# First-stage shift and scale from one-column matmuls, and seven units in the first stage instead of three

## The chip, the core and the metric

The kernel runs on one core of one Trainium2 chip. The core has a matrix engine (TensorE, PE in the rows; PEld is its loading of weights), a vector engine (VectorE, DVE), a scalar engine (ScalarE, ACT), GpSimd (POOL) and a queue that issues transfers (SyncE, SP). Each has its own instruction queue and runs it in order. The metric is device time in microseconds, from launch to end.

## The reference, cut to what matters

A decoder block of 256 tokens and width 2048: an FFN, a token mixer and a second FFN, each fed by a normed input that a shift and a scale modulate. All nine modulation vectors are one vector-matrix product.

```python
c_act = jax.nn.silu(c)                       # c: (1, 2048)
mod = c_act @ w_ada[l] + b_ada[l]            # w_ada: (2048, 9 * 2048)
sh1, sc1, g1, sh2, sc2, g2, sh3, sc3, g3 = jnp.split(mod, N_MOD, axis=-1)

h = modulate(rmsnorm(x, norm1_w[l]), sh1, sc1)        # rmsnorm(x) * (1 + sc1) + sh1
x = x + 0.5 * g1[:, None, :] * swiglu(h, ffn1_gate[l], ffn1_up[l], ffn1_down[l])
...
```

## The kernel before, in words

Everything is float32. A matmul of activations with a weight is made exact enough by splitting both operands into two float32r parts (`hi`, `lo`) and adding three products (lines 239 to 241). Weights come as panels `w` of 128 partitions x 1024 columns (two blocks of 128 rows by 512 output columns, 512 KB). For each panel ACT writes the `hi` half (L214) and DVE the `lo` half (L215) of a tile `hl`. A **unit** is a pair of PSUM banks (two token tiles) for one chunk of 512 gate or up columns; a **step** of a unit is one panel: 12 matmuls of 512 columns.

The transposed, modulated input `h` is needed in blocks of 128 features, and its shift (`s_col`) and scale (`a_col`) depend on `w_ada`. So the first FFN starts in **stages** of feature blocks, `STAGES = ((0, 2), (2, 4), (4, 8), (8, 12), (12, 16))`: stage s first needs the shift and scale of its blocks, then works through its units on those blocks alone. Partial sums stay in PSUM (`carry`), or are copied out by ACT to `part` (L517) and added to by DVE later (L524).

Shift and scale of a block come from `dot_panel` (L98): a 512 KB panel `at` of transposed `w_ada` (features on partitions, half of the 2048 inputs along the row) is multiplied with the row `crow` = silu(c) on DVE and summed along the row (L101). Two vectors, two halves: four panels to a block, eight for a stage of two blocks. `col_fin` (L105) adds halves, bias and 1 (L110 to L113). `crow` itself is made by four matmuls that spread one row over 128 partitions (`cb`, L89) and a Silu on ACT (L90).

`h_pre` normalises and transposes (tiles `xn`, `hx`, L307 and L312), `h_post` applies scale and shift and splits (L324, L325 on ACT, L328 on DVE).

What sets the order: a `Feed` queue holds the dot panels of the next stage; `mm_unit` pops some behind each weight panel, by a rate, and `next_stage` drains it but for two, issues the first weight panel of the next stage, and flushes the last two. All raw panels (`w`, `at`) share one ring of 7 buffers, all issued by SP in program order: an issue waits until its buffer was read. Split tiles `hl` have 5 buffers.

Stage 0 works on three units (the first two of `pairs` in reverse, and `res`), which stay in PSUM; rate is 0 there, so all eight dot panels of stage 1 are popped by `next_stage`. Stage 1 takes these three one step further and then eight more units two steps each. In all 3 + 19 = 22 steps.

Of the kernel before, what the change touches and what calls it, by code (L numbers as in the profile page):

```python
# [7 lines left out]
F32 = mybir.dt.float32  # L8
# [18 lines left out]
BEHIND = (3, 8, 16)  # L27
CARRY = 2
DEFER, YDEFER = 2, 4
# [13 lines left out]
def decoder_block(  # L43
    ctx: ExitStack,
    tc: tile.TileContext,
    x_in, c_t, c_r, ada_t, ada_g, b_row, b_col, norm_c, gate1, up1, down1, w_in, pool_w, pool_c,
    lb_c, gnorm, w_out, gate2, up2, down2, fin_w, ident_c, lmask_c, pcnt_c, out,
# [14 lines left out]

# [1 line left out]
    ccol = const.tile([P, KB], F32, name="ccol")  # L64
# [6 lines left out]
    ident = const.tile([P, P], F32, name="ident")  # L71
    nc.sync.dma_start(out=ident, in_=ident_c)
    bcol = const.tile([P, 9 * KB], F32, name="bcol")
    nc.sync.dma_start(out=bcol, in_=b_col)
    ncol = const.tile([P, 3 * KB], F32, name="ncol")
    nc.sync.dma_start(out=ncol, in_=norm_c)
    ones = const.tile([P, P], F32, name="ones")
# [17 lines left out]

# [1 line left out]
    # shift and scale: output features on partitions, one dot product over c per partition  # L97
    def dot_panel(vec, blk, half):  # L98
        raw = wraw.tile([P, AW], F32, tag="raw", name=f"at{vec}_{blk}_{half}")
        nc.sync.dma_start(out=raw, in_=ada_t[COLS.index(vec), blk, half])  # L100
        nc.vector.scalar_tensor_tensor(  # L101
            raw, raw, 1.0, crow[:, half * AW:(half + 1) * AW], ALU.mult, ALU.mult,
            accum_out=dots[:, COLS.index(vec), blk, half:half + 1])

    def col_fin(vec, b0, b1):  # L105
# [8 lines left out]

    # gates: input features on partitions, partial products summed over partitions by PE into every row
    def row_step(vec, half, k, box):
# [23 lines left out]
    class Feed:  # L140
# [3 lines left out]
        def add_blocks(self, vecs, b0, b1):  # L144
# [4 lines left out]
            for vec in vecs:  # L149
                self.q.append((0, lambda v=vec: col_fin(v, b0, b1), vecs[-1]))  # L150

        def add_row(self, vec):
            def begin():
                self.g[vec] = state.tile([P, D], F32, tag="g", name=f"g{vec}")
            self.q.append((0, begin, vec))
            for h in range(2):
                box = {}
                for k in range(KB):
                    self.q.append((1, lambda h=h, k=k, box=box: row_step(vec, h, k, box), vec))
                self.q.append((0, lambda h=h, box=box: row_fin(vec, h, box, self.g[vec]), vec))  # L160
# [22 lines left out]

# [1 line left out]
    cnt = [0]  # L185
# [35 lines left out]
    def mm_unit(ps, steps, rate, lag=0, first=True, last=True):  # L221
        """ps[t] = sum over steps (lhs(t) parts, panel source); token tile 1 trails by lag steps of 2 K blocks"""
        n = len(steps)
        held = {}
        if ahead:
            held[0] = ahead.pop()
        for i in range(n + lag):
            for t in range(NT):
                j = i - lag * t
                if not 0 <= j < n:  # L230
                    continue
                if j not in held:
                    held[j] = panel(steps[j][1], rate, lag > 0 and j % 3 == 2)
                if len(steps[j]) > 2:
                    ensure(steps[j][2])
                for b, (wh, wl) in enumerate(held[j]):
                    xh, xl = steps[j][0](b, t)
                    st, sp = first and j == 0 and b == 0, last and j == n - 1 and b == 1
                    nc.tensor.matmul(ps[t], xh, wh, start=st, stop=False)  # L239
                    nc.tensor.matmul(ps[t], xh, wl, start=False, stop=False)  # L240
                    nc.tensor.matmul(ps[t], xl, wh, start=False, stop=sp)  # L241
# [13 lines left out]

# [1 line left out]
    def rsqrt(ssq, n, denom, bias, name):  # L257
        """-2 / sqrt(ssq / denom + bias), the square root of ACT refined by a Newton step"""
        r = small.tile([P, n], F32, tag="rr", name=f"rr_{name}")
        m = small.tile([P, n], F32, tag="rq", name=f"rq_{name}")  # L260
        u = small.tile([P, n], F32, tag="ru", name=f"ru_{name}")
        a = nc.scalar.activation(r, ssq, AF.Sqrt, bias=bias, scale=1.0 / denom)
        nc.vector.tensor_scalar(m, ssq, 1.0 / denom, bias, ALU.mult, ALU.add)
        nc.vector.reciprocal(r, r)
        if n > 1:
            nc.vector.tensor_tensor(u, r, r, ALU.mult)
            nc.vector.tensor_tensor(u, u, m, ALU.mult)
        else:
# [23 lines left out]

# [48 lines left out]

# [1 line left out]
    def split_slot(slot, b, ps):  # L343
# [3 lines left out]
    def project(w, srcs, g_t, rate, name, y=None, first=False, ssq=None, then=None, post=None, need=None):  # L347
        """g_t given: x += g * (y + srcs @ w), then(t); else y (+)= srcs @ w"""
        rs = {}
# [50 lines left out]

# [1 line left out]
    def hid_chunk(name, sl, up, defer):  # L402
        """sl[t] <- sl[t] * up[t], transposed and split into a slot"""
        slot = slots.tile([P, 2, 4, S], F32R, tag="sl", name=f"hid{name}")
# [42 lines left out]

# [1 line left out]
    ssq = new_ssq("0")  # L449
    rstd = {}  # L450
    for t in range(NT):
        for n in range(4):
            add_ssq(ssq, t, n, n * CW, CW)
        rstd[t] = row_rstd(ssq, t, row_bias(ssq, t, "0"), "0", 3)
        nc.vector.tensor_scalar(rstd[t], rstd[t], -0.5, None, ALU.mult)

    def stage_pre(st):
        k0, k1 = STAGES[st]
        return [([k, k + 1], h_pre(0, rstd, [k, k + 1], [0, 1], True)) for k in range(k0, k1, 2)]

    pre = stage_pre(0)
    feed.add_blocks((1, 0), *STAGES[0])

    def next_stage(c, i, k):
        """the rest of the modulation that the next stage needs, its first weight panel a little before the end"""
        feed.drain(AHEAD)
        ahead.append(panel((gate1, up1)[i][c, k // 2], 0))
        feed.flush()
# [4 lines left out]
    def order(s):  # L473
        fin = s == len(STAGES) - 1
        units = pairs[::-1] if (len(STAGES) - s) % 2 == 0 else list(pairs)
        if s == 0:
            units = units[::-1][:CARRY]
        keep = [] if fin else units if s == 0 else units[-CARRY:]
        return units + res if fin or s == 0 else units[:CARRY] + res + units[CARRY:], keep

# [3 lines left out]
    for s, (k0, k1) in enumerate(STAGES):  # L484
# [9 lines left out]
        else:  # L494
            feed.add_blocks((1, 0), *STAGES[s + 1])
            rate = 2 * sum(c for c, _, _ in feed.q) / sum(k1 - at.get(u, 0) for u in units) if s else 0
        for c, i in units:
# [45 lines left out]

# [1 line left out]
    feed.add_row(8)  # L545
# [33 lines left out]
    def to_feat(src, name):  # L579
        """two [tok, 512] tiles -> two PSUM banks [feat, 2 blocks, tok]"""  # L580
        res = []
# [16 lines left out]
    def hgrn(g):  # L598
# [23 lines left out]
        def col_sums(ps, k_ap, q_ap, name, i):  # L622
            """every row of ps = sums over the partitions of k * q"""
            pr = tmp.tile([P, CW], F32, tag="ev", name=f"pr{g}_{name}")
# [134 lines left out]

# [1 line left out]
    ssq = new_ssq("3")  # L761
# [4 lines left out]
    def finish(t, rs):  # L766
        for n in (1, 0, 2, 3):
# [13 lines left out]

_NAMES = ["x", "c_t", "c_r", "ada_t", "ada_g", "b_row", "b_col", "norm_c", "gate1", "up1", "down1", "w_in", "pool_w", "pool_c",
          "lb_c", "gnorm", "w_out", "gate2", "up2", "down2", "fin_w", "ident", "lmask", "pcnt"]
# [59 lines left out]
```

## Time and profile before

| | |
|---|---|
| median of 3 runs | 1874.09 us (1873.69 to 1875.05) |
| the profiled execution: span | 1872.2 us |
| median less span (launch, end) | 1.9 us |
| PE busy | 1838.7 us (98% of the span) |
| DVE busy, ACT busy | 1368.6 us, 866.1 us |
| read from memory | 491.28 MB |
| first matmul of stage 0, of stage 1, of stage 2 | 26.33, 41.50, 97.35 us |

The span runs from the first to the last instruction of the one profiled execution; the times of runs lie about 1.9 us above it. PE's share is high because a matmul is counted from its start to the end of its pipeline, and the next starts before that end.

### The profile page before, as it was taken

To read this page: it belongs to the slowest core of one execution; us is meant where nothing else is said; L and a number is where in the kernel's file an instruction comes from. 1 tells how busy PE (TensorE), PEld (TensorE's weight loads), DVE (VectorE), ACT (ScalarE), POOL (GpSimd) and SP (SyncE) were. 2 spreads that over 40 slices of the span, in tenths; PEclk is the share of its full clock that TensorE was granted. 3 is DMA by queue.
4 is the path that set the end of the run, shared out by engine and by line. 5 is a ranking of instruction groups with operands and counts; after the bars stand their busy time and mean duration, and the time that the engine had idled before them with its cause. 6 is when DMAs were issued, how large, how long until landed. Compare 5 with 4: busy or idle time off the path is not lost.

```text
span 1872.2 us, 22892 instructions
## 1 busy us (share of the span) xinstructions
PE 1838.7 (98%) x8348; PEld 1516.6 (81%) x8348; DVE 1368.6 (73%) x1721; ACT 866.1 (46%) x1085; POOL 6.5 (0%) x12
## 2 busy tenths in 40 slices
PE   5999999999999999999999999999999999999997
PEld 3878888888888888788888887888888888888886
DVE  6789898778888778898898859875444444454466
ACT  5554555444434444644535446444444444334443
POOL 0000000000000000000000000000000000000000
PEclk9999999999999999999999999999999999999999
DMA  9999988999999998477868857996555555555552
GB/s 365 328 332 333 307 265 316 341 341 331 329 335 340 337 333 292 156 268 268 317 251 316 274 205 250 323 330 204 189 192 198 190 183 189 193 196 189 187 192 90
DMA packets 137678, 494.89 MB, mean 264 GB/s; under 512 B 15831, under 2 KB 17367, under 8 KB 137181
## 3 DMA queue, kind: packets, MB, share of 16 engines
q1 hardware_dynamic: 137566, 493.44, 75.2%
q8 instruction: 65, 1.06, 0.2%
q14 instruction: 47, 0.39, 0.1%
HBM read 491.28 MB, written 2.10 MB: 264 GB/s over the span
## 4 chain that ended last, share of the span: by engine, by line
PE 97%; DVE 2%; ACT 0%; issue 0%; DMA 0%; SPq 0%; DVEq 0%; ACTq 0%
PE d L241 8%; PE d L240 8%; PE d L239 8%; PE u L241 7%; PE u L239 7%; PE u L240 7%; PE g L240 6%; PE g L239 6%; PE g L241 6%; PE s L241 4%; PE s L239 4%; PE s L240 4%; PE wo L240 2%; PE wo L239 2%; PE wo L241 2%; PE ht L413 1%
## 5 line engine op out<-in xcount | busy, mean ns | idle before, releaser
L215 DVE TENSOR_TENSOR hl<-w,hl 128x1024 fp32r<-128x1024 f32 x640 | 779.4, 1222 | 416.0 <-ACT hl L214 414.4
L214 ACT CAST hl<-w 128x1024 fp32r<-128x1024 f32 x640 | 672.5, 1055 | 828.6 <-PE d L241 219.6
L239 PE MATMUL d<-hl,hid 128*128 128x512 f32 x704 | 274.5, 390 | 0.0
L240 PE MATMUL d<-hl,hid 128*128 128x512 f32 x704 | 274.0, 389 | 0.0
L241 PE MATMUL d<-hl,hid 128*128 128x512 f32 x704 | 274.0, 389 | 0.0
L101 DVE SCALAR_TENSOR_TENSOR at<-at,crow 128x1024 f32<-128x1024 f32 x192 | 233.1, 1217 | 1.5 <-DMA at<-in_ada_t 1.5
L239 PE MATMUL u<-hl,h 128*128 128x512 f32 x544 | 211.6, 389 | 0.0
L240 PE MATMUL u<-hl,h 128*128 128x512 f32 x544 | 211.6, 389 | 0.0
L241 PE MATMUL u<-hl,h 128*128 128x512 f32 x544 | 211.6, 389 | 0.0
L239 PE MATMUL g<-hl,h 128*128 128x512 f32 x512 | 200.6, 392 | 0.0
L240 PE MATMUL g<-hl,h 128*128 128x512 f32 x512 | 199.6, 390 | 0.0
L241 PE MATMUL g<-hl,h 128*128 128x512 f32 x512 | 199.3, 390 | 0.0
L241 PEld LDWEIGHTS d<-hl,hid 128*128 128x128 f32 x704 | 132.1, 188 | 27.6
L240 PEld LDWEIGHTS d<-hl,hid 128*128 128x128 f32 x704 | 132.2, 188 | 27.2
L239 PEld LDWEIGHTS d<-hl,hid 128*128 128x128 f32 x704 | 132.1, 188 | 27.1
L239 PE MATMUL s<-hl,h 128*128 128x512 f32 x320 | 127.3, 398 | 12.3 <-ACT h L324 12.3
L240 PE MATMUL s<-hl,h 128*128 128x512 f32 x320 | 126.2, 394 | 0.0
L125 DVE SCALAR_TENSOR_TENSOR acc<-ag,ccol,acc 128x1024 f32<-128x1024 f32 x96 | 122.7, 1278 | 4.1 <-DMA ag<-in_ada_g 3.6
L241 PE MATMUL s<-hl,h 128*128 128x512 f32 x320 | 124.7, 395 | 0.9 <-DVE h L328 0.9
L240 PEld LDWEIGHTS u<-hl,h 128*128 128x128 f32 x544 | 102.1, 188 | 21.2
L241 PEld LDWEIGHTS u<-hl,h 128*128 128x128 f32 x544 | 102.1, 188 | 21.2
L239 PEld LDWEIGHTS u<-hl,h 128*128 128x128 f32 x544 | 102.1, 188 | 21.2
(247 smaller groups left out, 2035.6 us busy)
## 6 DMA issues: line engine op xcount, KB each, us to landing
at<-in_ada_t SPq DMA_DIRECT2D x192, 512.0 KB, 5.3
w<-in_up SPq DMA_DIRECT2D x176, 512.0 KB, 4.5
w<-in_gate SPq DMA_DIRECT2D x176, 512.0 KB, 4.7
w<-in_down SPq DMA_DIRECT2D x176, 512.0 KB, 3.8
ag<-in_ada_g SPq DMA_DIRECT2D x96, 512.0 KB, 5.1
w<-in_w_in SPq DMA_DIRECT2D x80, 512.0 KB, 4.7
w<-in_w_out SPq DMA_DIRECT2D x32, 512.0 KB, 4.5
x_sb<-in_x SPq DMA_DIRECT2D x2, 1024.0 KB, 7.0
```

Source lines behind the costliest of these rows:

```text
L101: nc.vector.scalar_tensor_tensor(raw, raw, 1.0, crow[:, half * AW:(half + 1) * AW], ALU.mult, ALU.mult, accum_out=dots[:, COLS.index(vec), ...
L125: nc.vector.scalar_tensor_tensor(acc, raw, ccol[:, k:k + 1], acc, ALU.mult, ALU.add)
L214: nc.scalar.copy(hl[:, 0], raw)
L215: nc.vector.tensor_tensor(hl[:, 1], raw, hl[:, 0].bitcast(F32), ALU.subtract)
L239: nc.tensor.matmul(ps[t], xh, wh, start=st, stop=False)
L240: nc.tensor.matmul(ps[t], xh, wl, start=False, stop=False)
L241: nc.tensor.matmul(ps[t], xl, wh, start=False, stop=sp)
L413: nc.tensor.transpose(ps[:, i, t * P:(t + 1) * P], sl[t][:, (b + i) * P:(b + i + 1) * P], ident)
```

## The change

Shift and scale of the first stage's two blocks are computed on TensorE: panels `as` (plain `w_ada` blocks, eight of 512 KB like before) serve as weights for one-column matmuls with a column of `ccol` = silu(c), 8 to a panel and 16 accumulated for each of four columns (2 vectors x 2 blocks) of one PSUM tile `a0`. `crow` is still made, for the later stages. Stage 0 takes seven units: four that are copied out to `part` afterwards (`SPILL`), then `res`, then the two that stay in PSUM. Stage 1 then has 15 steps instead of 19 (7 + 15 = 22), and its feed rate applies in stage 0 as well. Beside that, three small transfers are issued by ACT instead of SP, the second token tile's squares are summed by DVE in two instructions of 1024 instead of four on ACT, and one square root serves both tiles.

```diff
-CARRY = 2
+CARRY, SPILL = 2, 4
...
-    nc.sync.dma_start(out=ident, in_=ident_c)
+    nc.scalar.dma_start(out=ident, in_=ident_c)
...
+    first_ps = ps_ms.tile([P, 2, STAGES[0][1]], F32, tag="ms", name="a0")
+
+    def dot_pe(vi, blk, half):
+        raw = wraw.tile([P, KB // 2, P], F32, tag="raw", name=f"as{vi}_{blk}_{half}")
+        nc.sync.dma_start(out=raw, in_=ada_s[vi, blk, half])
+        for i in range(KB // 2):
+            k = half * (KB // 2) + i
+            nc.tensor.matmul(first_ps[:, vi, blk:blk + 1], raw[:, i, :], ccol[:, k:k + 1],
+                             start=k == 0, stop=k == KB - 1)
+
+    def col_fin_pe(vi, vec):
+        n = STAGES[0][1]
+        res = (s_col if vec == 0 else a_col)[:, 0, 0:n]
+        nc.vector.tensor_tensor(res, first_ps[:, vi, :], bcol[:, vec * KB:vec * KB + n], ALU.add)
+        if vec == 1:
+            nc.vector.scalar_tensor_tensor(res, res, 1.0, ncol[:, 0:n], ALU.add, ALU.mult)
...
-    rstd = {}
-    for t in range(NT):
-        for n in range(4):
-            add_ssq(ssq, t, n, n * CW, CW)
-        rstd[t] = row_rstd(ssq, t, row_bias(ssq, t, "0"), "0", 3)
-        nc.vector.tensor_scalar(rstd[t], rstd[t], -0.5, None, ALU.mult)
+    for n in range(4):
+        add_ssq(ssq, 0, n, n * CW, CW)
+    for n in range(2):
+        junk = slots.tile([P, 2, AW], F32, tag="sl", name=f"sq{n}")
+        xs = x_sb[:, 1, n * AW:(n + 1) * AW]
+        nc.vector.scalar_tensor_tensor(junk[:, 0], xs, 1.0, xs, ALU.mult, ALU.mult, accum_out=ssq[:, 1, n:n + 1])
...
+    feed.add_first()
+    feed.drain(4)
     pre = stage_pre(0)
-    feed.add_blocks((1, 0), *STAGES[0])
...
         if s == 0:
-            units = units[::-1][:CARRY]
-        keep = [] if fin else units if s == 0 else units[-CARRY:]
-        return units + res if fin or s == 0 else units[:CARRY] + res + units[CARRY:], keep
+            units = units[::-1]
+            return units[CARRY:CARRY + SPILL] + res + units[:CARRY], units[:CARRY]
+        keep = [] if fin else units[-CARRY:]
+        return units + res if fin else units[:CARRY] + res + units[CARRY:], keep
...
-            rate = 2 * sum(c for c, _, _ in feed.q) / sum(k1 - at.get(u, 0) for u in units) if s else 0
+            rate = 2 * sum(c for c, _, _ in feed.q) / sum(k1 - at.get(u, 0) for u in units)
```

The order of TensorE's queue at the start of the program, before (`cb` are the matmuls that spread c, `hx` the transposes, `s` the units; a row's x4 or x8 counts equal instructions in sequence):

```order
L89 MATMUL cb_117<-c_87,ones 128x512
L312 MATMUL hx_0_0_166<-ident,xn_0_0_165 128x128 x4
L239 MATMUL s_4_1_0_213<-hl_193,h_0_164 128x512
L240 MATMUL s_4_1_0_213<-hl_193,h_0_164 128x512
L239 MATMUL s_4_1_1_214<-hl_193,h_0_164 128x512
```

And after the change (`a` is the PSUM tile of the shifts and scales, `as` its panels of `w_ada`):

```order
L89 MATMUL cb_117<-c_87,ones 128x512
L113 MATMUL a_123<-ccol,as_0_0_150 128x1 x8
L113 MATMUL a_123<-ccol,as_0_1_160 128x1 x8
L113 MATMUL a_123<-ccol,as_1_0_170 128x1 x8
L337 MATMUL hx_0_0_192<-ident,xn_0_0_191 128x128 x4
L113 MATMUL a_123<-ccol,as_1_1_180 128x1 x8
L113 MATMUL a_123<-ccol,as_0_0_201 128x1 x8
L113 MATMUL a_123<-ccol,as_0_1_211 128x1 x8
L113 MATMUL a_123<-ccol,as_1_0_226 128x1 x8
L113 MATMUL a_123<-ccol,as_1_1_236 128x1 x8
L264 MATMUL s_3_1_0_253<-hl_223,h_0_190 128x512
```

64 one-column matmuls stand between the last `cb` and the first matmul of a unit, in the place of nothing but the transposes.

The order of VectorE's queue where stage 0 ends, before (from the split of the third unit's panel to the split of `h` for stage 1):

```order
L215 TENSOR_TENSOR hl_250<-w_248,hl_250 128x1024
L101 SCALAR_TENSOR_TENSOR at_2_1_277,dots<-at_2_1_277,crow 128x1024
L101 SCALAR_TENSOR_TENSOR at_2_0_280,dots<-at_2_0_280,crow 128x1024
L101 SCALAR_TENSOR_TENSOR at_2_1_283,dots<-at_2_1_283,crow 128x1024
L101 SCALAR_TENSOR_TENSOR at_3_0_286,dots<-at_3_0_286,crow 128x1024
L101 SCALAR_TENSOR_TENSOR at_3_1_289,dots<-at_3_1_289,crow 128x1024
L110 TENSOR_TENSOR a_col<-dots 128x2
L111 TENSOR_TENSOR a_col<-a_col,bcol 128x2
L113 SCALAR_TENSOR_TENSOR a_col<-a_col,ncol 128x2
L215 TENSOR_TENSOR hl_294<-w_292,hl_294 128x1024
L101 SCALAR_TENSOR_TENSOR at_3_0_297,dots<-at_3_0_297,crow 128x1024
L101 SCALAR_TENSOR_TENSOR at_3_1_300,dots<-at_3_1_300,crow 128x1024
```

And after (from the split of the seventh unit's panel):

```order
L240 TENSOR_TENSOR hl_391<-w_389,hl_391 128x1024
L101 SCALAR_TENSOR_TENSOR at_3_1_394,dots<-at_3_1_394,crow 128x1024
L128 TENSOR_TENSOR a_col<-dots 128x2
L129 TENSOR_TENSOR a_col<-a_col,bcol 128x2
L131 SCALAR_TENSOR_TENSOR a_col<-a_col,ncol 128x2
L240 TENSOR_TENSOR hl_420<-w_418,hl_420 128x1024
L101 SCALAR_TENSOR_TENSOR at_3_0_423,dots<-at_3_0_423,crow 128x1024
L101 SCALAR_TENSOR_TENSOR at_3_1_426,dots<-at_3_1_426,crow 128x1024
L128 TENSOR_TENSOR s_col<-dots 128x2
L129 TENSOR_TENSOR s_col<-s_col,bcol 128x2
```

Five dot panels of stage 1 now stand between the splits of stage 0 instead of behind its last one; the last three, with a split between them, are where they were.

## Rows read from the trace of the kernel before

**Rows 1.** The page, part 1: busy time and share of the engines.

```profile
PE 1838.7 (98%) x8348; PEld 1516.6 (81%) x8348; DVE 1368.6 (73%) x1721; ACT 866.1 (46%) x1085; POOL 6.5 (0%) x12
```

**Rows 2.** Waits of PE, whole span: total us, times, longest us.

```profile
PE s L239 <- ACT h L324: 12.3, 5, 7.3
PE hx L312 <- ACT xn L307: 7.4, 2, 5.1
```

**Rows 3.** Chain that ended last, first 45 us: start us, us, what.

```profile
3.15 7.17 PE cb L89 x8
...
17.77 3.44 DVE at L101 x6
...
25.45 0.17 DVE s_col L111
...
38.10 2.30 DVE at L101 x4
...
40.63 0.17 DVE s_col L111
```

**Rows 4.** Timeline, stages 0 and 1: start us, duration us, what, idle before.

```profile
15.45 0.69 PE L312 MATMUL hx<-ident,xn 128*128 128x128 f32 x2 [5.14 <-ACT xn L307]
...
26.33 0.80 PE L239 MATMUL s<-hl,h 128*128 128x512 f32 x1 [7.27 <-ACT h L324]
...
27.35 0.63 PE L239 MATMUL s<-hl,h 128*128 128x512 f32 x1
...
31.28 0.39 PE L240 MATMUL s<-hl,h 128*128 128x512 f32 x1
...
41.50 0.79 PE L239 MATMUL s<-hl,h 128*128 128x512 f32 x1 [4.38 <-ACT h L324]
```

**Rows 5.** Stretches: PE busy (count), PEld, DVE, ACT, POOL, granted clock, DMA, GB/s.

```profile
20.00:30.00 10.00, 3.66 (x8) 2.46 (x9) 8.91 (x19) 4.71 (x8) 0.00 (x0) 1.00 1.02 408
...
37.00:41.50 4.50, 0.12 (x3) 0.00 (x1) 4.43 (x8) 1.67 (x3) 0.00 (x0) 0.85 1.00 396
41.50:47.00 5.50, 5.48 (x12) 3.90 (x13) 4.49 (x6) 4.86 (x9) 0.00 (x0) 0.50 1.01 409
47.00:95.90 48.90, 48.90 (x217) 40.44 (x217) 37.00 (x53) 25.24 (x33) 0.00 (x0) 1.00 0.93 331
```

**Rows 6.** Tile cb: count, ns min/median/max, first and last start us.

```profile
L89 PEld LDWEIGHTS cb<-c,ones x8: 281/332/332, 3.1 to 8.4; 1*128 1x128 f32 x8
L89 PE MATMUL cb<-c,ones x8: 1056/1056/1186, 3.1 to 9.2; 1*128 1x512 f32 x8
```

**Rows 7.** Weight loads by shape, whole span: count, busy us, mean ns, idle.

```profile
L239 PEld LDWEIGHTS d<-hl,hid 128*128 128x128 f32 x704 | 132.1, 188 | 27.1
...
L653 PEld LDWEIGHTS pl<-kk 128*126 128x126 f32 x32 | 3.8, 189 | 0.2
...
L653 PEld LDWEIGHTS pl<-kk 128*64 128x64 f32 x32 | 2.0, 138 | 0.7 <-issue 0.4 <-PE zi L241 0.4
```

**Rows 8.** Timeline of PE in the mixer: start us, duration us, what.

```profile
832.61 1.87 PE L653 MATMUL pl<-kk 128*126 128x64 f32 x16
...
845.92 1.69 PE L653 MATMUL pl<-kk 128*112 128x64 f32 x16
```

**Rows 9.** Groups of DVE, first 200 us: count, busy us, mean ns, idle before.

```profile
L215 DVE TENSOR_TENSOR hl<-w,hl 128x1024 fp32r<-128x1024 f32 x61 | 73.8, 1221 | 14.2 <-ACT hl L214 14.1
L101 DVE SCALAR_TENSOR_TENSOR at<-at,crow 128x1024 f32<-128x1024 f32 x59 | 71.3, 1218 | 0.0
L524 DVE TENSOR_TENSOR part<-s,part 128x512 f32<-128x512 f32 x24 | 16.4, 688 | 6.1 <-PE s L241 6.1
```

**Rows 10.** Timeline where stage 1 ends: start us, duration us, what, idle before.

```profile
95.68 0.16 DVE L111 TENSOR_TENSOR s_col<-s_col,bcol 128x4 f32<-128x4 f32 x1
...
95.86 0.40 PE L241 MATMUL s<-hl,h 128*128 128x512 f32 x1
...
97.35 0.50 PE L239 MATMUL s<-hl,h 128*128 128x512 f32 x1 [0.22 <-ACT h L324]
```

More of the change, by code (lines that the diff above doesn't have):

```diff
@@ L45, in decoder_block @@
     tc: tile.TileContext,
-    x_in, c_t, c_r, ada_t, ada_g, b_row, b_col, norm_c, gate1, up1, down1, w_in, pool_w, pool_c,
+    x_in, c_t, c_r, ada_s, ada_t, ada_g, b_row, b_col, norm_c, gate1, up1, down1, w_in, pool_w, pool_c,
     lb_c, gnorm, w_out, gate2, up2, down2, fin_w, ident_c, lmask_c, pcnt_c, out,
@@ L71, in decoder_block @@
     ident = const.tile([P, P], F32, name="ident")
-    nc.sync.dma_start(out=ident, in_=ident_c)
+    nc.scalar.dma_start(out=ident, in_=ident_c)
     bcol = const.tile([P, 9 * KB], F32, name="bcol")
-    nc.sync.dma_start(out=bcol, in_=b_col)
+    nc.scalar.dma_start(out=bcol, in_=b_col)
     ncol = const.tile([P, 3 * KB], F32, name="ncol")
-    nc.sync.dma_start(out=ncol, in_=norm_c)
+    nc.scalar.dma_start(out=ncol, in_=norm_c)
     ones = const.tile([P, P], F32, name="ones")
@@ L150, in add_blocks, with add_first @@
                 self.q.append((0, lambda v=vec: col_fin(v, b0, b1), vecs[-1]))
+        def add_first(self):
+            for vi, vec in enumerate((1, 0)):
+                for b in range(STAGES[0][1]):
+                    for h in range(2):
+                        self.q.append((1, lambda vi=vi, b=b, h=h: dot_pe(vi, b, h), 0))
+                self.q.append((0, lambda vi=vi, vec=vec: col_fin_pe(vi, vec), 0))
         def add_row(self, vec):
@@ L449, in decoder_block @@
     ssq = new_ssq("0")
-    rstd = {}
-    for t in range(NT):
-        for n in range(4):
-            add_ssq(ssq, t, n, n * CW, CW)
-        rstd[t] = row_rstd(ssq, t, row_bias(ssq, t, "0"), "0", 3)
-        nc.vector.tensor_scalar(rstd[t], rstd[t], -0.5, None, ALU.mult)
+    for n in range(4):
[4 more added lines that the diff above has]
+        nc.vector.scalar_tensor_tensor(junk[:, 0], xs, 1.0, xs, ALU.mult, ALU.mult, accum_out=ssq[:, 1, n:n + 1])
+    tot = small.tile([P, NT], F32, tag="tot", name="tot")
+    nc.vector.tensor_reduce(tot[:, 0:1], ssq[:, 0, 0:4], AX.X, ALU.add)
+    nc.vector.tensor_reduce(tot[:, 1:2], ssq[:, 1, 0:2], AX.X, ALU.add)
+    r0 = rsqrt(tot, NT, D, eps, "0")
+    nc.vector.tensor_scalar(r0, r0, -0.5, None, ALU.mult)
+    rstd = {t: r0[:, t:t + 1] for t in range(NT)}
     def stage_pre(st):
@@ L780, in decoder_block @@
         lambda t, cs: nc.vector.tensor_tensor(x_sb[:, t, cs], x_sb[:, t, cs], fw[:, cs], ALU.mult))
-_NAMES = ["x", "c_t", "c_r", "ada_t", "ada_g", "b_row", "b_col", "norm_c", "gate1", "up1", "down1", "w_in", "pool_w", "pool_c",
+_NAMES = ["x", "c_t", "c_r", "ada_s", "ada_t", "ada_g", "b_row", "b_col", "norm_c", "gate1", "up1", "down1", "w_in", "pool_w", "pool_c",
           "lb_c", "gnorm", "w_out", "gate2", "up2", "down2", "fin_w", "ident", "lmask", "pcnt"]
@@ L801 @@
     ada_t = np.stack([w_ada[:, v * D:(v + 1) * D].T.reshape(KB, P, 2, AW).transpose(0, 2, 1, 3) for v in COLS])
+    ada_s = np.stack([w_ada[:, v * D:v * D + STAGES[0][1] * P].reshape(2, KB // 2, P, -1, P).transpose(3, 0, 2, 1, 4)
+                      for v in (1, 0)])
     ada_g = np.stack([w_ada[:, v * D:(v + 1) * D].reshape(KB, P, 2, AW).transpose(2, 0, 1, 3) for v in ROWS])
@@ L815 @@
         "c_r": i["c"].reshape(1, D),
-        "ada_t": ada_t, "ada_g": ada_g,
+        "ada_s": ada_s, "ada_t": ada_t, "ada_g": ada_g,
         "b_row": i["b_ada"].reshape(1, 9 * D),
```

## The prediction

> **What bounds the kernel now.** I read the page first: PE is busy 98% of the span [rows 1], so only what PE waits for, or does in addition, can change the time. PE's own list of waits comes next: 12.3 us in front of units' first matmuls for the modulated `h`, 7.4 us for the normed input [rows 2], nearly all before 42 us. So the change is worth what it does to the first 100 us, and behind stage 1 the two kernels run the same work.
>
> The chain of the first 45 us shows what those waits consist of. PE spreads c until 3.15 + 7.17 = 10.32; then a run of dot panels on VectorE ends in the shift of stage 0 at 25.62, and another in that of stage 1 at 40.80 [rows 3]. The timeline has the first matmul of stage 0 at 26.33, 0.7 us behind the shift, and that of stage 1 at 41.50 after 4.4 us of idle PE [rows 4]. Stage 1's first step is slow as well: for 5.5 us the granted clock is 0.50, the lower of the two levels, 1.2 GHz [rows 5]. Stage 2 starts with almost no wait, at 97.35 [rows 10]. Transfers run at about 408 GB/s from 20 to 30 us [rows 5], 1.28 us for a panel of 512 KB.
>
> In that light the change has two promises: start stage 0 earlier by taking dot products off VectorE, and hide stage 1's dot panels under seven units. I check each.
>
> **The dot products on PE.** There are 2 vectors x 2 blocks x 16 = 64 one-column matmuls. A plain float32 matmul leaves two records: the four `cb` instructions left eight matmuls and eight weight loads [rows 6]. So 128 pairs of load and matmul. With one column to stream, the pace is that of the loads of 128 x 128 weights, which no row shows alone. The nearest rows are the mixer's `pl` matmuls, float32 with weights of 126 and 112 columns and 64 streamed columns, 16 records in a run. The run's duration less about 0.27 for the last record, over 15: (1.87 - 0.27) / 15 = 107 ns for 126 columns and (1.69 - 0.26) / 15 = 95 ns for 112 [rows 8]. That is 0.85 ns to a column, about two cycles of 2.4 GHz, and the load's own duration agrees: 189 ns for 126 and 138 for 64, 0.82 to a column [rows 7]. For 128 columns: 109 ns, at the upper clock.
>
> Which clock will PE have there? The matmuls before it, `cb`, run back to back for 7.2 us; the start-to-start of its records is 7.17 / 8 = 0.90 us for 512 columns twice, 1024 cycles: 0.85 us at 1.2 GHz, 0.43 at 2.4. They are at the lower level to their end, whatever the clock column prints that early (it prints 1.00 until a first change is recorded: the units' matmuls of 0.63 us at 27.35 are like that too, and 0.39 at 31.28 [rows 4]). So the one-column matmuls begin at the lower level, and rows that resemble them most, small-operand float32 matmuls right before them, did not lift it. I take the lower level for all of them. Does the load follow the clock? In `cb` a load of 128 columns takes 281 to 332 ns [rows 6] against 188 [rows 7]: 188 less its column part of 107 is 81, and 81 + 2 x 107 = 295 lies in that range. So yes: 213 ns a pair, 128 x 0.213 = 27.3 us. Bounds: 128 x 0.109 = 14.0 us if the clock rises or the load doesn't follow it, 128 x 0.332 = 42.5 us if successive loads at the lower level don't overlap at all. I take 27.3, since the column arithmetic fits both levels. The four transposes between them add 0.9 us, from two in 0.69 [rows 4].
>
> The Trainium skill, "TensorE: Matmul & The Clock Gate", section "LDWEIGHTS (loading the stationary operand)", gives the load as columns / 1.2 ns, 107 ns for 128, with no second figure for the lower clock. By it the phase would take 13.7 us instead of 27.3. The mixer's rows agree with it at the upper clock; those of `cb` speak against it at the lower.
>
> **Term 1, start of stage 0.** 10.32 + 27.3 + 0.9 = 38.5; result and bias add on DVE 0.4; 0.7 from shift to first matmul as before: 39.6 against 26.33, **+13.3 us**. No transfer is later than that: x and eight panels, 6.3 MB, pass by about 20 us at 0.41 MB/us, and the ring lets go of a buffer every 3.4 us. SP waits for PE's reading behind the seventh transfer, and weight panels queue behind it, but three panels and two dot panels have landed by 39. The earlier statistics (four Squares fewer on ACT, two DVE sums of 1.2 us, one square root), the three transfers on ACT's queue and SP's earlier issue are covered: the normed input is wanted by PE only behind the third `as` panel, at 10.3 + 3 x 3.4 = 20.5, where before it was there by 18.4 us; uncovered, it would cost at most the 2 us that two sums take. VectorE waits for PE's last panel from about 25 to 38.7, as the dot panels of stage 1 are queued behind the shift; nothing of the removed 9 us of dot products comes back as time.
>
> **Term 2, stage 0 to 1.** Seven units are 84 matmuls at 48.9 / 217 = 0.225 us [rows 5], 19 us, with 1.9 for the slow first ones, 0.5 for transposes and 0.4 for the `lo` half of `h`: PE ends at 61.4. DVE splits the seventh panel just ahead of that unit (58.8, as ACT casts a panel only behind its copies of the unit two before). Behind that stand a dot panel, the scale, a split, two dot panels and the shift: 4 x 1.15 + 1.0 = 5.6 (four panels' worth in steps of 1.15, from 2.30 for two [rows 3]): 64.4. Stage 1 starts at 65.1, after an idle of 3.7 instead of 4.4: **-0.7 us**. The wait is not hidden because what precedes it still includes three transfers' worth of DVE work that program order puts last. The restart at the lower clock stays. Bounds: 0, and -7 if the idle goes and the restart with it (4.4 + half of 5.5).
>
> **Term 3, stage 1 to 2.** PE does four steps fewer (the moved ones, neutral), but DVE now adds four spilled units into `part`: 8 x 0.69 = 5.5 us [rows 9]. From shift to shift it has 15 splits and 16 dot panels, 31 x 1.15 = 35.6, the adds, 1.5 for small ones, and waits for ACT like before (14.1 in 200 us [rows 9], some 3 here): 45.6, to 110.0, and PE could start stage 2 at 110.7. PE's own work: 65.1 + 180 x 0.225 = 40.5, + 2.6 for the low clock and 0.4: 108.6, then 1.3 of transposes and start as before (95.86 + 0.23 to 97.35 [rows 10]): 109.9. DVE ends last: **+0.8 us**, bounds 0 and +3.
>
> **Sum.** 13.3 - 0.7 + 0.8 = +13.4; directly, stage 2 starts at 110.7 instead of 97.35. On the execution's own time: 1872.2 + 1.9 = 1874.1, which is also the median; + 13.4 gives 1887.5, rounded **1888 us**. With the bounds of terms 2 and 3 the case spans +6 to +18: 1880 to 1892.
>
> **Rivals.** 0.2% is 3.7 us, about what a measurement of this kernel can tell from no change.
>
> (a) *Upper clock or a load that ignores the clock*: 109 ns a pair. Term 1 becomes 10.3 + 14.0 + 0.6 + 0.4 + 0.7 = 26.0, -0.3, and up to 1.9 less for a fast start; the other terms stay: between -1.6 and +0.4, 1872.5 to 1875. For it: nothing before this stretch shows PE streaming through full 128-row operands, so its level there is not in a row. Against: `cb`. This is also what the skill's rule gives.
>
> (b) *Faster: VectorE's work vanishes under the seven units.* Given (a), if DVE runs a step ahead of PE in stage 0, its last dot panels end before PE's last unit; the idle of 4.4 us and the slow restart of 2.75 go. -0.3 - 1.9 - 7.1 = -9.3: 1865. It decides from the point where the shift of stage 1 is there 0.7 us before PE ends the seventh unit, 4.4 us earlier than I work out. For it: 15 x 1.15 = 17.3 us of panels are less than the 19 us of seven units. Against: the casts wait in ACT's queue for the copies of a unit, so the splits cannot run ahead, and dot panels stand behind the splits. A variant, pairs at the transfers' pace (1.28 / 16 = 80 ns or less), starts stage 0 at 22.3 and comes to about 1869; 95 ns for 112 columns speaks against it.
>
> (c) *Loads that don't overlap* at the lower clock: +29 us, 1903. The 107 ns of a 189 ns load [rows 7, 8] speak against.
>
> **Chances.** The forecast 0.72; (a) 0.13; (b) with its variant 0.10; (c) 0.05. Faster by over 0.2%: 0.10. Within: 0.13. Slower: 0.77. The range leaves out (b) and (c), 0.15, and runs from (a)'s lower end to the forecast's upper with 2 us for a longer pair: 1872 to 1894. The forecast's own range is 1880 to 1892.
>
> **What the profile would show.** Right: `a0` matmuls from 10.3 to about 38 us in an even pace of 0.43 us per instruction; first unit near 39.6; VectorE idle for some 13 us before; an idle of 3 to 4 us near 62; stage 2 near 111. Wrong in term 1: the `a0` phase over by 25 us, or held by transfers. Wrong in term 2: no gap and no slow clock before stage 1. A change in any row behind stage 2's start would mean that something else moved.

## The result, and the profile after the change

The changed kernel takes 1891.68 us (median; 1891.11 to 1892.22) against 1873.89 for the kernel before, run beside it on the same chip: ratio 1.0095, 95% interval 1.0083 to 1.0107. That is 17.8 us slower, where the prediction said 13.9 (1888 from 1874.1), inside its range. Span of the profiled execution: 1890.4 us, 18.2 more than before.

The page's part 1 and PE's list of waits, whole span, answer to [rows 1, 2]:

```profile
PE 1869.1 (99%) x8476; PEld 1546.9 (82%) x8476; DVE 1366.0 (72%) x1709; ACT 864.0 (46%) x1076; POOL 6.4 (0%) x12
```

```profile
PE s L264 <- ACT h L349: 7.0, 5, 3.0
PE cb L89 <- DMA c<-in_c_r: 3.0, 1, 3.0
```

PE waits less for `h` than before (7.0 us against 12.3), no longer for the normed input (7.4 before), and is busy 30 us more: the wait ahead of stage 0 has become work. 128 records more, 64 one-column matmuls of two records each, account for 27.4 us of it. The chain of the first 45 us, which answers to [rows 3], shows that work as what sets the start:

```profile
2.40 8.06 DMA as<-in_ada_s
...
10.60 10.37 PE a L113 x48
20.98 0.96 PE hx L337 x4
21.93 3.22 PE a L113 x16
25.39 13.83 PE a L113 x64
39.24 0.17 DVE s_col L119
39.43 0.57 ACT h L349
```

PE waits some 0.5 us for the first panel and starts at 10.60, 0.28 us behind the end of `cb` in [rows 3]. VectorE's first shift now comes at 39.24 (25.45 before). The 128 records take 27.42 us, 0.214 each. Loads and matmuls of the tile `a`, whose rows list count, then ns at least, in the middle and at most, show loads 1.8 times as long as the 188 ns of [rows 7], for weights of the same 128 x 128:

```profile
L113 PEld LDWEIGHTS a<-ccol,as x128: 288/333/338, 10.6 to 38.8; 128*128 128x128 f32 x128
L113 PE MATMUL a<-ccol,as x128: 212/352/373, 10.6 to 38.8; 128*128 128x1 f32 x128
```

The timeline of PE at the starts of stages 0, 1 and 2 answers to [rows 4, 10] (start, duration, idle before):

```profile
40.05 0.79 PE L264 MATMUL s<-hl,h 128*128 128x512 f32 x1 [0.85 <-ACT h L349]
...
66.14 0.50 PE L264 MATMUL s<-hl,h 128*128 128x512 f32 x1 [2.98 <-ACT h L349]
...
105.19 0.39 PE L266 MATMUL s<-hl,h 128*128 128x512 f32 x1
...
109.72 0.39 PE L266 MATMUL s<-hl,h 128*128 128x512 f32 x1
112.87 0.50 PE L264 MATMUL s<-hl,h 128*128 128x512 f32 x1 [2.76 <-ACT h L349]
```

From 105.19 to 109.72 lie twenty starts, 0.227 us to a matmul, so 10.9 us to the 48 matmuls that the four spilled units move from stage 1 to stage 0. Stretches of the same time answer to [rows 5]: PE busy (count), PEld, DVE, ACT, POOL, granted clock, DMA share, GB/s.

```profile
40.05:46.10 6.05, 6.03 (x13) 4.30 (x14) 3.26 (x5) 4.72 (x9) 0.00 (x0) 1.00 0.58 189
...
66.10:70.00 3.90, 3.80 (x9) 2.56 (x10) 3.03 (x5) 3.89 (x8) 0.00 (x0) 0.56 1.03 409
70.00:109.90 39.90, 39.90 (x181) 32.77 (x179) 36.23 (x52) 17.74 (x22) 0.00 (x0) 1.00 0.94 340
...
114.40:121.00 6.60, 6.04 (x14) 4.79 (x15) 5.84 (x8) 4.68 (x9) 0.00 (x0) 0.50 0.93 339
121.00:170.00 49.00, 49.00 (x217) 40.53 (x217) 42.57 (x55) 22.16 (x24) 0.00 (x0) 1.00 0.91 321
```

Two things were not in the prediction. Stage 2 now waits 2.76 us (0.22 before) and runs at the lower clock for some 7 us behind that wait. And stage 0 starts slowly for 6 us, 13 matmuls where full speed has 26, though the column prints 1.00 there: no change of clock has been recorded yet.

The table gives, for this kernel and most that follow, the time of the first `h` of stage 0 on ACT's timeline, the distances from there to the first `h` of the next stages, and the median time. The two kernels that issue panels faster are left out, because the first `h` of stage 3 is there before PE wants it and its mark says nothing of PE. In e4 the same holds for stage 1. Moving four units shifts 10.9 us from "1 to 2" into "0 to 1", moving three shifts 8.2.

| kernel | stage 0 | 0 to 1 | 1 to 2 | 2 to 3 | time, us |
|---|---|---|---|---|---|
| before | 25.71 | 15.17 | 55.85 | 62.43 | 1873.89 |
| after | 39.43 | 26.10 | 46.72 | 65.29 | 1891.68 |
| e1, matmuls only | 39.79 | 16.64 | 55.96 | 62.43 | 1889.65 |
| e2, units only | 24.42 | 22.05 | 46.35 | 64.51 | 1872.55 |
| e6, neither (new norm) | 24.30 | 15.58 | 56.88 | 62.45 | 1873.13 |
| e3, half the matmuls | 25.79 | 25.33 | 46.46 | 65.18 | 1878.22 |
| e4, clock lifted twice | 50.30 | 16.68 | 47.32 | 62.41 | 1891.39 (one run) |
| e11, clock lifted once | 46.61 | 26.28 | 46.83 | 63.78 | 1898.30 (one run) |
| e5, wait filled | 39.71 | 25.32 | 47.93 | 62.45 | 1890.05 |
| e8, no additions | 39.81 | 25.82 | 45.60 | 64.05 | 1890.07 |
| six units, VectorE's dots | 24.14 | 19.74 | 47.42 | 62.44 | 1869.06 |

After less before, with the 10.9 us taken out: +13.7 at stage 0, 0.0 to stage 1, +1.8 to stage 2, +2.9 to stage 3: 18.4. From there on the two traces run alike (stage 4 begins at 220.71 and 239.07, 18.4 apart; the spans differ by 18.2).

### The profile page after: what moved, and what is told of

It is laid out like the page before. It is cut to its first block, busy times and chain, and to the rows that moved or that the text cites. A ratio compares the mean times of both kernels' runs of the same rounds, so it can differ in the third digit from the quotient of the medians.

```text
span 1890.4 us, 23133 instructions
## 1 busy us (share of the span) xinstructions
PE 1869.1 (99%) x8476; PEld 1546.9 (82%) x8476; DVE 1366.0 (72%) x1709; ACT 864.0 (46%) x1076; POOL 6.4 (0%) x12
## 4 chain that ended last, share of the span: by engine, by line
PE 98%; DVE 1%; DMA 0%; ACT 0%; issue 0%; SPq 0%; DVEq 0%
PE d L264 8%; PE d L265 8%; PE d L266 8%; PE u L266 7%; PE u L265 7%; PE u L264 7%; PE g L265 6%; PE g L264 6%; PE g L266 6%; PE s L266 4%; PE s L264 4%; PE s L265 4%; PE wo L266 2%; PE wo L264 2%; PE wo L265 2%; PE a L113 1%
## 5 line engine op out<-in xcount | busy, mean ns | idle before, releaser
L101 DVE SCALAR_TENSOR_TENSOR at<-at,crow 128x1024 f32<-128x1024 f32 x184 | 224.1, 1219 | 0.5 <-DMA at<-in_ada_t 0.5
L266 PEld LDWEIGHTS d<-hl,hid 128*128 128x128 f32 x704 | 132.2, 188 | 27.4
```

Of the source, the lines that this page charges most:

```text
L101: nc.vector.scalar_tensor_tensor(raw, raw, 1.0, crow[:, half * AW:(half + 1) * AW], ALU.mult, ALU.mult, accum_out=dots[:, COLS.index(vec), ...
```

## The experiments

The kernel before was run beside each on the same chip, at 1873.98 to 1874.31 us.

### One part alone: e1 and e2

e1 keeps the one-column matmuls and goes back to three units with no feed in stage 0:

```diff
-            return units[CARRY:CARRY + SPILL] + res + units[:CARRY], units[:CARRY]
+            return units[:CARRY] + res, units[:CARRY]
...
-            rate = 2 * sum(c for c, _, _ in feed.q) / sum(k1 - at.get(u, 0) for u in units)
+            rate = 2 * sum(c for c, _, _ in feed.q) / sum(k1 - at.get(u, 0) for u in units) if s else 0
```

> One part alone: the one-column matmuls on TensorE stay, stage 0 works on the old three units, with no panels of stage 1 pushed into it. My theory: the start of stage 0 is as late as in the changed kernel (first matmul near 40 us, +13.7), and without the four added units nothing is moved into the cover; stage 1 then loses a little to the missing cover, stage 2's first matmul comes near 111.9 against 97.4 before, and the time is about 1888 us (+14, range 1885 to 1891). The wait ahead of stage 2 should be small again (under 1 us), with no new fall of the clock there. Rival, that the seven units make the changed kernel slow and the one-column matmuls cost little: 1874 to 1878 us here.

Measured: 1889.65 us (1889.39 to 1890.33), ratio 1.0086 [1.0071, 1.0101]. Timeline of PE, first matmul of stages 0, 1 and 2:

```profile
40.41 0.79 PE L264 MATMUL s<-hl,h 128*128 128x512 f32 x1 [0.85 <-ACT h L349]
57.05 0.80 PE L264 MATMUL s<-hl,h 128*128 128x512 f32 x1 [5.08 <-ACT h L349]
...
113.01 0.50 PE L264 MATMUL s<-hl,h 128*128 128x512 f32 x1 [0.22 <-ACT h L349]
```

The start is as late as in the changed kernel, the wait ahead of stage 2 is back at 0.22, and stage 2 takes the 62.43 us of before. So the matmuls, with the new first norm, cost 15.7 us, and the wait with its restart belongs to the units.

e2 keeps the seven units and takes the dot products from VectorE:

```diff
-    feed.add_first()
-    feed.drain(4)
     pre = stage_pre(0)
+    feed.add_blocks((1, 0), *STAGES[0])
```

> The other part alone: shift and scale of stage 0 come from VectorE again, with the seven units of the changed kernel. My theory: stage 0 starts at 25 to 27 us as before; the wait ahead of stage 1 falls from 4.4 us to about 1; the wait ahead of stage 2 (0.2 us before, 2.8 in the changed kernel) stays near 2.9 with its restart at the lower clock, so that about as much is lost there as is won: 1871 to 1876 us, 1873 the likeliest. Rival, that the seven units alone are what makes the changed kernel slow: 1888 us or more. Rival, that the units take the whole wait ahead of stage 1 away and nothing comes in its place: 1869 us or less.

Measured: 1872.55 us (1870.22 to 1874.25), ratio 0.9993 [0.9983, 1.0002]. On PE:

```profile
25.04 0.79 PE L264 MATMUL s<-hl,h 128*128 128x512 f32 x1 [5.63 <-ACT h L349]
47.08 0.50 PE L264 MATMUL s<-hl,h 128*128 128x512 f32 x1 [0.66 <-ACT h L349]
...
93.44 0.80 PE L264 MATMUL s<-hl,h 128*128 128x512 f32 x1 [2.75 <-ACT h L349]
```

Here the units hide nearly all of stage 1's panels (0.66 us of wait for 4.38). Stage 2 then waits 2.75 us and restarts at the lower clock, as in the changed kernel. By the table, 5.3 us have been gained by the start of stage 1, 3.9 are left at stage 2 and 1.8 at stage 3. Units alone are no measurable change.

### The new first norm alone: e6

Both parts undone (the edits of e1 and e2 together).

> The changed kernel with both parts undone: shift and scale of stage 0 from VectorE, three units in stage 0. What stays of the change is the rewritten first norm (one norm for both token tiles, two of its squares on VectorE). Asked is what that alone is worth, since the seven-unit version started stage 0 1.3 us earlier than the kernel before. Theory: the start at about 25.0 us instead of 26.3 is the norm's, and all behind it moves with it: about 1872.8 us (1871.5 to 1874), 1.2 us below before. Rival, that the start comes from the units: 26.3 us and no change, 1874.2 us.

Measured: 1873.13 us (1871.63 to 1874.27), ratio 0.9996 [0.9987, 1.0004]. Stage 0 does begin 1.4 us earlier, so the earlier start in e2 is the norm's. But the table shows it gone at stage 2 (96.76 against 96.73 before): the expectation that all behind moves along was wrong, and the median, 0.9 us lower, cannot tell either way.

### Half the one-column matmuls: e3

```diff
-        for i in range(KB // 2):
+        for i in range(0, KB // 2, 2):
...
-                             start=k == 0, stop=k == KB - 1)
+                             start=k == 0, stop=k == KB - 2)
```

> Leaves out half of stage 0's dot products (the odd one of every two input blocks), so 32 one-column matmuls instead of 64, the same transfers, all else as in the changed kernel. My theory, that the matmuls' own pace at the lower clock (two records of 0.213 us each) sets stage 0's start: 32 x 2 x 0.213 = 13.6 us go, first matmul of stage 0 near 26.4 us, time about 1878 us (1876 to 1880). Rival, that the transfers of the eight panels or the chain behind them set the start: it stays above 36 us and the time above 1888 us.

Measured: 1878.22 us (1877.50 to 1878.68), ratio 1.0022 [1.0013, 1.0032]. PE's timeline:

```profile
18.57 6.99 PE L113 MATMUL a<-ccol,as 128*128 128x1 f32 x32 [0.25 <-DVE a_col L119]
26.41 0.79 PE L264 MATMUL s<-hl,h 128*128 128x512 f32 x1 [0.85 <-ACT h L349]
```

64 records fewer, with the same transfers, bring the start 13.6 us forward, 0.213 us a record, and the time 13.5. The transfers, which are the same, set nothing behind the first panel.

### The clock under the one-column matmuls: e4 and e11

e4 puts wide matmuls ahead of `cb`, and more among the last four panels:

```diff
+    wide = ones_r.unsqueeze(1).broadcast_to([P, 4, P])
+    hold = ps_mm.tile([P, CW], F32, tag="mm", name="hold")
+    for _ in range(24):
+        nc.tensor.matmul(hold.rearrange("p (a b) -> p a b", a=4), ones_r, wide, start=True, stop=True)
...
+            if vi == 1 and i % 2:
+                nc.tensor.matmul(hold, raw[:, i, :], x_sb[:, 0, 0:CW], start=True, stop=True)
```

> Adds 24 matmuls of 512 columns ahead of the first matmuls, to bring the granted clock up before the one-column matmuls, and in the last four of the eight panels one float32 matmul of 512 columns behind every second one-column matmul, so that the engine is kept busy there (added work, results unused; its whole time is of no interest). Asked are the pace of the one-column matmuls and the granted clock. My theory: the pace is that of the weight load and goes with the clock, so at the upper level a record of the one-column matmul takes about 0.11 us (half of 0.213), and the load's record 188 ns or less against 333. Open to me is whether the level holds through the bare one-column matmuls of the first four panels; if it falls there, the pace goes back to 0.213 us, and the changed kernel's low clock is what its own matmuls leave. Rival, that the pace does not depend on the clock: 0.21 us at either level.

`cb` on its timeline, and its stretches:

```profile
8.70 4.02 PE L93 MATMUL cb<-c,ones 1*128 1x512 f32 x8
```

```profile
4.00:12.00 8.00, 8.00 (x27) 5.01 (x25) 2.15 (x3) 2.14 (x6) 0.00 (x0) 1.00 0.99 404
12.00:30.00 18.00, 17.75 (x75) 16.17 (x75) 4.09 (x14) 7.04 (x14) 0.00 (x0) 0.50 0.66 244
33.00:50.00 17.00, 17.00 (x80) 10.79 (x80) 2.37 (x3) 2.09 (x2) 0.00 (x0) 1.00 0.53 190
```

The first wide matmuls lifted the clock, for the records of `cb` behind them start 0.50 us apart where before they took 0.90; but it fell at 12 us, while PE ran `cb`, before the first one-column matmul at 12.65; under these it stayed at 0.50, and rose only among the wide matmuls of the last four panels. e11 therefore places its wide matmuls directly ahead of the first one-column matmul:

```diff
+    hold = ps_mm.tile([P, CW], F32, tag="mm", name="hold")
...
+            if vi + blk + half + i == 0:
+                for _ in range(10):
+                    nc.tensor.matmul(hold, raw[:, i, :], x_sb[:, 0, 0:CW], start=True, stop=True)
```

> The changed kernel with 10 float32 matmuls of 512 columns (results unused) between the arrival of the first panel and the first one-column matmul, so that the clock is at its upper level directly ahead of the 64 bare one-column matmuls; whole time of no interest. Asked is whether they hold the level themselves. My theory, that they leave the clock low by themselves: after the wide ones the granted clock is 1.00, the first one-column records go at 0.09 to 0.11 us each, and within the row of them the clock falls to 0.50 and their pace to 0.213 us; stage 0 starts 4 us or less earlier than the wide matmuls' own length says. Rival, that the low clock in the changed kernel is only inherited from the idle engine before: it stays at 1.00 to the end of the row, and the 128 records take 14 us or less in place of 27.6.

Chain of e11, the loads of the tile `a` (ns at least, in the middle and at most), then stretches of `a` alone (PE, PEld and DVE, clock, DMA share, GB/s):

```profile
22.31 9.67 PE a L117 x64
31.98 0.95 PE hx L341 x4
32.94 13.46 PE a L117 x64
```

```profile
L117 PEld LDWEIGHTS a<-ccol,as x128: 190/333/338, 21.7 to 46.0; 128*128 128x128 f32 x128
```

```profile
22.15:24.15 2.00, 2.00 (x19) 2.00 (x18) 0.00 (x0) 1.00 0.00 0
24.15:26.15 2.00, 2.00 (x20) 2.00 (x19) 0.00 (x0) 1.00 0.53 174
26.15:27.00 0.85, 0.85 (x7) 0.85 (x6) 0.00 (x0) 0.61 0.88 251
27.00:29.00 2.00, 2.00 (x11) 2.00 (x10) 0.00 (x0) 0.50 0.74 242
```

The first records run at the upper level, 19 or 20 to 2 us. Then the level falls to 0.50 with PE never idle, and 11 records take 2 us (a record at either edge counts in both stretches). The mean of 0.61 puts the fall at 26.34. The 64 records of the first row are 5.64 us at the lower level, 26.4 records at 0.214, and 4.03 us at the upper for the other 37.6: 0.107 us each. The loads do the same: 190 to 192 ns each from 22.1 to 25.9, 333 from 26.9 on. So the pace follows the clock, and the one-column matmuls do not hold the upper level. Both questions are answered as the forecast assumed.

The two kernels bear on stage 0 as well. In e4, where the clock is still up when stage 0 begins, PE works through seven units without idling ahead of stage 1: first matmul to first matmul is 19.7 us (50.91 to 70.61), against 26.09 in the changed kernel. In e11 stage 0 begins 7 us later than in the changed kernel, but at the lower clock, and it takes the same 26.28 us with the same wait of 2.97. So a later start alone does not shorten stage 0. That the clock alone does is not shown, because VectorE's queue is in another order in e4: three splits and two dot panels stand ahead of the shift of stage 0 (27.52 to 42.2 us), where the changed kernel and e11 have a single split.

### What stands behind the start of stage 2: e5, e8, e9

e5 fills the wait there with matmuls of zero weights:

```diff
+    zero_r = const.tile([P, P], F32R, name="zero_r")
+    nc.vector.tensor_scalar(zero_r, ones, 0.0, None, ALU.mult)
...
+            if s == 2 and (c, i) == units[0]:
+                for _ in range(13):
+                    nc.tensor.matmul(ps[0], zero_r, ahead[0][0][1], start=False, stop=False)
```

> Asked is what of term 3's miss is the wait ahead of stage 2 and what the restart at the lower clock behind it. The changed kernel, with 13 matmuls of 512 columns with zero weights put into that wait (they add nothing to the sums; their panel is there before the wait begins). The wait itself cannot get shorter by it. If the restart costs 2.8 us of its own, as the later stage marks of the changed kernel say, the granted clock stays up behind stage 2's start, stage 3 starts about 2.8 us earlier against stage 2's start, and the time is about 1889 us (1888 to 1890). Rival, that the time goes in the wait alone and the low clock behind it is hidden by other waits: 1891.5 us, no change.

Measured: 1890.05 us (1889.68 to 1890.57), ratio 1.0087 [1.0073, 1.0101]; 1.6 us less than the changed kernel, where 2.7 were expected. PE's timeline, and a stretch:

```profile
110.71 3.11 PE L540 MATMUL s<-hl,zero_r 128*128 128x512 f32 x13
113.66 0.42 PE L266 MATMUL s<-hl,h 128*128 128x512 f32 x1
```

```profile
113.00:121.00 8.00, 7.10 (x31) 5.45 (x30) 6.89 (x8) 7.82 (x15) 0.00 (x0) 1.00 0.99 375
```

The clock stays up, and stage 2 takes 62.45 us, as before the change, instead of 65.29: the restart is worth 2.8 us by itself. Of the missing 1 us, 0.7 lies ahead of the edit: in this execution the low clock at stage 1's start lasted from 65.2 to 72.0 instead of 66.5 to 69.9 and 1 to 2 took 1.2 us more, so that stage 2 begins at 112.96 instead of 112.25. Why that stretch differs is open.

e8 leaves out the eight additions of stage 1 (`else:` becomes `elif s != 1:` ahead of the addition to `part`):

> The changed kernel without stage 1's eight additions into the parts (it leaves those sums out): the part of term 3 that the prediction named as what VectorE gets more to do. Theory now: VectorE's last dot panel, and with it the wait ahead of stage 2, hangs on the whole row of panels and splits that are spread over stage 1, of which the additions are the smaller part: the wait falls only from 2.8 to about 2 us and the time to about 1890.7 (1889 to 1891.5). Theory of the prediction, that the additions are what makes VectorE late: 8 x 0.69 = 5.5 us less work, more than the wait, so the wait and the restart go and the time is 1886 to 1887 us.

Measured: 1890.07 us (1889.68 to 1891.58), ratio 1.0088 [1.0074, 1.0102]. The wait is 1.83 us:

```profile
111.85 0.50 PE L264 MATMUL s<-hl,h 128*128 128x512 f32 x1 [1.83 <-ACT h L349]
```

5.5 us less of work on VectorE shorten stage 1 by 1.1 us. So the additions are the smaller part of what makes VectorE late. Its timeline in the changed kernel shows the larger:

```profile
107.68 0.08 DVE L101 DVE_READ_ACCUMULATOR at<-at,crow 128x1 f32 x1
...
108.30 1.22 DVE L240 TENSOR_TENSOR hl<-w,hl 128x1024 fp32r<-128x1024 f32 x1
109.45 1.22 DVE L101 SCALAR_TENSOR_TENSOR at<-at,crow 128x1024 f32<-128x1024 f32 x1
...
110.59 1.22 DVE L101 SCALAR_TENSOR_TENSOR at<-at,crow 128x1024 f32<-128x1024 f32 x1
...
112.05 0.16 DVE L129 TENSOR_TENSOR s_col<-s_col,bcol 128x4 f32<-128x4 f32 x1
```

PE is done at 110.11. The split at 108.30 and the two dot panels behind it run one after another until 111.8, and only then comes the shift. e9 issues the panels faster, in this stage and the others, so that fewer stand at the end:

```diff
-            rate = 2 * sum(c for c, _, _ in feed.q) / sum(k1 - at.get(u, 0) for u in units)
+            rate = 2.3 * sum(c for c, _, _ in feed.q) / sum(k1 - at.get(u, 0) for u in units)
```

> The changed kernel with the dot panels of the next stage issued faster (factor 2.3 for 2 in the rate), so that the last panel is not left for the end of a stage. Theory: the wait ahead of stage 2 falls from 2.8 to about 0.6 us with some 2 us of waits for weight panels inside stage 1 in its place, and the restart behind it goes; the time is about 1888.5 us (1887.5 to 1890). Rival, that VectorE has too much work in stage 1 in any order: no change, 1891 to 1892.5 us.

Measured: 1888.24 us (1886.03 to 1889.74), ratio 1.0076 [1.0062, 1.0090], 3.4 us less than the changed kernel. PE:

```profile
65.61 0.50 PE L264 MATMUL s<-hl,h 128*128 128x512 f32 x1 [1.87 <-ACT h L349]
86.98 0.50 PE L265 MATMUL s<-hl,h 128*128 128x512 f32 x1 [1.78 <-DVE hl L240]
```

The wait moves into stage 1 (1.78 us for a split at 86.98), the clock stays up at stage 2, and the restart is saved. By the first `h` on ACT's timeline stage 2 begins 1.6 us earlier than in the changed kernel (110.62 against 112.25) and stage 4 3.7 us earlier (235.37 against 239.07). No work was taken from VectorE, only its order changed: the last panels had been put too late.

### Versions below both: six and five units

Dot products on VectorE as in e2, with `SPILL` 3 (six units in stage 0), and with `SPILL` 2 (five units) and the faster issue of e9:

```diff
-CARRY, SPILL = 2, 4
+CARRY, SPILL = 2, 3
```

> A version to beat both: shift and scale from VectorE as before the change, and six units in stage 0 instead of three or seven. Theory: stage 0 starts at 25 to 27 us as before, most of the wait ahead of stage 1 (4.4 us) goes, and with one unit less moved than in the seven-unit version the wait ahead of stage 2 stays near 1.2 us, too short to bring the clock down: about 1869 us (1867 to 1871.5), 0.2 to 0.3 per cent below before. Rival, that the clock falls behind the wait all the same: 1872 us.

> A second version to beat both, beside the six-unit one: shift and scale from VectorE, five units in stage 0, and the dot panels issued faster (factor 2.3 for 2). Theory: the faster issue takes the rest of the wait ahead of stage 2 (1 us there in the six-unit version), one unit less leaves some more ahead of stage 1: about 1868.5 us (1867 to 1871), the same as the six-unit version within 1 us.

Measured: six units 1869.06 us (1868.42 to 1872.49), ratio 0.9979 [0.9970, 0.9988]; five units with faster issue 1868.06 us (1867.02 to 1868.69), ratio 0.9967 [0.9955, 0.9979]. With six units stage 1 waits 1.23 us and stage 2 0.99 us, and no fall of the clock is recorded at either. The trace is of the fastest of eleven runs: seven lie between 1868.4 and 1869.3 us, four between 1871.3 and 1872.5, and whether the clock fell in those four is not recorded. With five, stage 1 waits 2.42 us and restarts at the lower clock, for 3.4 us; at stage 2 there is no such wait. Both beat the kernel before; which of them is better by 1 us the intervals don't settle. With VectorE's dot products, fewer units than seven bring 5 to 6 us in all, the new norm among it.

## Why the prediction was right, and where its sum was off

**What bounds the kernel.** Right: all differences lie ahead of stage 3, and behind it the rows run alike. The prediction named a change behind stage 2's start as the sign that something else moved, and that sign came: the restart there, below.

**Term 1, start of stage 0: +13.3 forecast, +13.7 measured.** The pace was to be 213 ns at the lower clock and is 214, and half the matmuls take half the time (e3). The two assumptions under it, that the clock is low there and that the load follows it, hold: 0.107 us at the upper level (e11), 0.214 at the lower. The rule cited from the Trainium skill, "TensorE: Matmul & The Clock Gate", section "LDWEIGHTS (loading the stationary operand)", gives columns / 1.2 ns, by estimate 107 ns for 128 columns. The trace agrees at the upper level alone; here the measurement decides, and the phase takes 27.4 us, not 13.7. Rival (a) needs the upper clock or a load that ignores it, and fails on both; rival (c), loads that do not overlap, fails on the pace. "No transfer is later" was not quite right: of the 0.4 us missing, 0.28 is the wait for the first panel. And the load as a fixed 81 ns and a part that doubles, 295 ns, was too short for the single load (333), which did no harm to the pace.

**Term 2, stage 0 to 1: -0.7 forecast, 0.0 measured.** The wait fell from 4.38 to 2.98, more than forecast, but the slow start of stage 0 gives it back: 13 matmuls take 6.05 us, 3.1 more than at full speed, where 1.9 had been put in. Why the units hide less here than in e2 is to be seen on VectorE, first the changed kernel, then e2:

```profile
41.40 0.69 DVE L353 TENSOR_TENSOR h<-h,h 128x512 fp32r<-128x512 f32 x1 [2.00 <-ACT h L350]
...
45.82 1.23 DVE L240 TENSOR_TENSOR hl<-w,hl 128x1024 fp32r<-128x1024 f32 x1 [1.45 <-ACT hl L239]
...
50.62 1.23 DVE L240 TENSOR_TENSOR hl<-w,hl 128x1024 fp32r<-128x1024 f32 x1 [2.44 <-ACT hl L239]
```

```profile
24.24 1.22 DVE L240 TENSOR_TENSOR hl<-w,hl 128x1024 fp32r<-128x1024 f32 x1
...
26.53 0.69 DVE L353 TENSOR_TENSOR h<-h,h 128x512 fp32r<-128x512 f32 x1
28.11 1.23 DVE L240 TENSOR_TENSOR hl<-w,hl 128x1024 fp32r<-128x1024 f32 x1 [0.89 <-ACT hl L239]
```

From the shift of stage 0 to that of stage 1 VectorE does the same work in both, but it idles 6.9 us in the changed kernel and 2.7 in e2. Of the 4.2 between, 2.0 are a matter of order: in the changed kernel the split of `h` stands at the head of the queue and waits for ACT, where in e2 a split and a dot panel stand ahead of it. The rest are waits for ACT's casts, which stand in ACT's queue behind copies of units that PE finishes late. That the low clock, here for 6 us and in e2 until 28.3, is behind these waits is argued from the timelines; no run has the changed kernel's order at the upper clock. The prediction had the casts waiting for copies and so kept the wait; the head of the queue and the longer slow start it did not see. So the one-column matmuls cost more than the 13.7 us of term 1. Apart, the parts change the time by +15.7 (e1) and -1.4 (e2), 14.3 together, with the new norm counted in both; joined, by 17.8. By the table some 3 us of what lies between arise in stage 0: the matmuls add 4.1 us to it under seven units (26.10 against 22.05) and 1.1 under three (e1 against e6).

**Term 3, stage 1 to 2: +0.8 forecast, +1.8 measured, and 2.9 more behind stage 2's start.** This term was mis-sized, and one was missing. VectorE does end last, as forecast, but its shift is there at 112.2 instead of 110.0, PE waits 2.76 us instead of the 0.8 worked out, and the prediction priced no restart at the lower clock, 2.8 us (e5). Its reason was wrong in part, too: it added eight additions in full, and they matter 1.1 of 5.5 us (e8). What ends late is the split and two panels that VectorE's queue holds last (e9). The prediction had used that very argument for term 2, and did not ask it again of stage 1.

**The range.** The bounds of the three terms add up to +6.3 and +16.3. The +18 written beside them is not their sum, and no term backs it. The measured +17.8 lies above 16.3, by the restart that had no term; that the range held it was luck.

**Rivals (a) and (b).** The sum of (a), redone with its own terms, is -2.1 to -0.2 instead of -1.6 to +0.4; nothing hangs on it. Rival (b), VectorE's work vanishing under the seven units, nearly happens when the matmuls are away (0.66 us of wait left in e2) and does in e4, with part of VectorE's panels done ahead of the stage, so its mechanism exists. The gain of 9.3 us that it promised does not, as stage 2's wait and restart take back 3.5 us in e2.

## What to carry to other kernels

In float32 a one-column matmul left two records here and went at the pace of its weight loads, and a row of them fell to half the clock even right behind wide matmuls: price such a phase at the lower level, and the start of whatever follows it. When work is moved between stages, do the sum of who ends last for every stage that gains or loses some, and give each wait that opens the price of a possible restart. Look also at what stands at the head and at the end of each engine's queue, since an edit elsewhere can change that order. Tune the split by the stage where the next wait opens: six units with VectorE's dot products gave 5 us where seven gave 1.4 or nothing.

## What the runs showed of the hardware that was not expected

The granted clock fell under a PE that was busy without a gap, on one-column matmuls (e11, at 26.34 us) and on `cb`, matmuls of one row of weights (e4, at 12 us). The low stretch behind a short wait lasted 3.4 us in some places (e8, stages 1 and 2) and 6.8 us in others (changed kernel, stage 2); what decides between them is open. The shorter ones cost 1.4 and 1.6 us by the table's last distances (e11, e8, stage 2), the longer ones 2.1 and 2.9 (e2, changed kernel). And the length of a wait alone does not decide whether it brings one: 2.38 us ahead of stage 2 in e4 left the clock up, while 1.83 in e8 and 2.76 in the changed kernel did not.
